# Gate units of the second layer: all 512-column matmuls in a row, then all of 256 columns

## The chip, the cores and the metric

The kernel runs on one core of a Trainium2 chip. The metric is device time in microseconds (us) of one execution. TensorE does matmuls, VectorE (DVE), ScalarE (ACT) and GpSimd (POOL) do elementwise work, and SyncE (SP) issues most DMAs.

## The reference

Two residual layers work on a sequence of 256 positions and 2048 features, with a context of 256 more positions. The first layer mixes with a Fourier transform, the second with windowed attention that also sees the context. Each ends with a gate: the mixed result is multiplied by silu(z), where z is a projection of the layer's normed input, and then projected back.

```python
D_MODEL, SEQ, DEPTH, D_BRANCH = 2048, 256, 2, 4096
def _attention_branch(h, hc, w_in, sink, rows, cols, need_ctx):
    q, k, v, z = jnp.split(h @ w_in, [D_BRANCH, D_BRANCH + kvw, D_BRANCH + 2 * kvw], axis=-1)
    ...
    y = jnp.moveaxis(o, 0, 1).reshape(b, n, D_BRANCH) * jax.nn.silu(z)
...
x = x + gate * (y @ w_out[i])
return _rmsnorm(x, final_g)
```

Here z of the second layer is h (256 x 2048) times the last 4096 columns of w_in.

## The kernel before

All matmuls run in fp32r, a reduced form of fp32. To keep precision, an fp32 operand is split into a high part and a low part (high = cast of the value, low = value minus high), and a product is made from three partial products: high x high, high x low, low x high. The helper `mm3` (lines 78 to 81 of the profile) does this with three matmuls of 512 columns. The helper `half_split`, or `w_cast` and `w_low` apart, split a weight tile of 128 x 1024: ScalarE casts the high part `wh` (L69, in the second layer L1086), VectorE subtracts to get the low part `wl` (L70, L1092).

The second layer is written as a list of units. There are `q` units (queries), `z` units (the gate) and `o` units (the first columns of the output projection). `emit_unit` emits the next unit's matmuls. A gate block `n` (there are 32) makes 128 of the 4096 columns of z for all 256 positions and consists of two `z` units, i = 0 and 1, each over 8 of the 16 tiles of 128 input features. Both units accumulate in one PSUM tile `o[0]` of 128 x 512. The activations `hx1[k]` are 128 x 512: the first 256 columns hold the high part of the 256 positions, the last 256 the low part. So for each k a unit issues two matmuls instead of three. One has wh as its stationary operand and moves all 512 columns (wh x high and wh x low, side by side in PSUM). The other has wl and moves the 256 high columns. `finish_z` later adds the two halves and applies the gate's function.

Matmul by matmul, the unit's loop alternates: k by k first the 512-column one (L1142), then the 256-column one (L1144). Only at the last k of the block is the pair turned, so that the last matmul of the block is the one that covers the whole tile and closes the accumulation.

From the eleventh unit on the order of TensorE, VectorE and ScalarE is written out by hand (`tc.manual_schedule`). A loop runs over 64 attention heads `i`. In it `s_max` (L1182), `s_exp` (L1191), `s_norm` (L1200) and `x_turn` (L1212) are the softmax on VectorE and ScalarE, `s_mm` issues the four score matmuls of the next head (L1173, L1174), `stage_o` the many small matmuls with the values (L1219), and `emit_unit` one or two units per head. `w_cast` and `w_low` prepare weights two to three units ahead. wh and wl share a pool `ws` of six buffers, and three units on, a wh takes the buffer of the wh before. In a group of four gate blocks the fourth block has four transposes (L1015, from `q_turn`) between its two units, in seven of the eight groups; in the other 25 blocks the second unit follows the first without anything between on TensorE. Behind each block stand the four score matmuls.

Behind the loop the remaining output columns are computed. There the order is the scheduler's own, which works with estimated times. `evac` moves a finished PSUM tile out (L1312 to L1314).

Of the kernel before, what the change touches and what calls it, by code (L numbers as in the profile page):

```python
# [16 lines left out]
P = 128  # L17
D = 2048
KT = D // P
DB = 4096  # L20
NB = DB // P
N = 256
# [7 lines left out]
def tile_dit(ctx: ExitStack, tc: tile.TileContext, a: dict, out: bass.AP):  # L30
    nc = tc.nc
    V, S, PE, GP = nc.vector, nc.scalar, nc.tensor, nc.gpsimd
# [8 lines left out]
    def psum():  # L41
        return pp.tile([P, 512], F32, tag="ps", name="ps")
# [35 lines left out]
    def mm3(o, wh, wl, xh, xl, start, stop):  # L78
        PE.matmul(o, wh, xh, start=start, stop=False)  # L79
        PE.matmul(o, wh, xl, start=False, stop=False)  # L80
        return PE.matmul(o, wl, xh, start=False, stop=stop).ins  # L81
# [98 lines left out]
    with tc.tile_pool(name="st", reuse_waits="tile", bufs=1, side="right") as st, ExitStack() as sts:  # L180
# [307 lines left out]
        for i in range(4):  # L488
            for j in range(4):
                k = 4 * i + j  # L490
# [188 lines left out]
    with tc.tile_pool(name="yp", reuse_waits="tile", bufs=32) as ypool:  # L679
# [19 lines left out]
        with tc.tile_pool(name="zp", reuse_waits="tile", bufs=2) as zp:  # L699
# [11 lines left out]
            for kg in range(4):  # L711
# [8 lines left out]
                for j in range(4):  # L720
                    k = kg * 4 + j
                    for b in range(4):
                        wh, wl = w[b // 2]
                        q = slice((b % 2) * 512 + j * P, (b % 2) * 512 + (j + 1) * P)
# [11 lines left out]
            for b in range(NE + 4, NB):  # L736
# [3 lines left out]
                o = psum()  # L740
                for k in range(KT):
                    wh, wl = w[k // 8]
                    q = slice((k % 8) * P, (k % 8 + 1) * P)
# [37 lines left out]
        for i in range(32):  # L781
            sw, kg = i // 16, i % 16
            if kg == 0:
                o = [psum() for _ in range(8)]
# [18 lines left out]
            for j, b in [(j, b) for b in range(8) for j in range(2)] if edge else [(j, b) for j in range(2) for b in range(8)]:  # L803
                q = slice(b * P, (b + 1) * P)
# [21 lines left out]
    o = psum()  # L826
# [12 lines left out]
    o = psum()  # L839
# [17 lines left out]
    for s in range(2):  # L857
        o = psum()[:, 0:N]
# [28 lines left out]
    with tc.tile_pool(name="h1", reuse_waits="tile", bufs=16) as h1p:  # L887
        hx1 = []
        kT = []
        with tc.tile_pool(name="kvp", reuse_waits="tile", bufs=2) as kvp:  # L890
            hc1 = []
            for k in range(KT):
# [3 lines left out]
                for s, h in ((0, hx), (1, hc)):  # L896
                    q = slice(s * N, (s + 1) * N)
# [10 lines left out]
            o = [[psum() for _ in range(2)] for _ in range(4)]  # L908
            for kg in range(8):
                w = [(kv_h, kv_l)] if kg == 0 else ws_split(raw(a["wkv"][kg]))  # L910
                for j in range(2):
                    k = kg * 2 + j
# [3 lines left out]
                    wh, wl = w[j]  # L916
                    for tb in range(4):
                        h = (hx1, hc1)[tb // 2][k]
                        c = (tb % 2) * P
                        for kv in range(2):  # L920
                            q = slice(kv * 512, (kv + 1) * 512)
# [13 lines left out]
            for hp in range(4):  # L935
                o = psum()
# [10 lines left out]
        with tc.tile_pool(name="ye", reuse_waits="tile", bufs=6) as yep, ExitStack() as ats:  # L947
# [23 lines left out]
            def o1_step(k, os_, wh, wl):  # L971
                while len(yh) <= min(k + 2, NB - 1) and (len(yh) < 28 or fin):
                    y_split(len(yh))
                for tb in range(2):
                    mm3(os_[tb], yh[k][:, tb * P : (tb + 1) * P], yh[k][:, N + tb * P : N + (tb + 1) * P], wh, wl, k == 0, k == NB - 1)
# [14 lines left out]
            def finish_q(hk, oq):  # L990
                qr = []
                for tb in range(2):
                    t = act()
                    if hk == 0:
                        roped(t, oq[tb], tb, actp, "act")
                    else:
                        t0 = act()
                        S.copy(t0, oq[tb])
                        roped(t, t0, tb, actp, "act", GP)
                    qr.append(t)  # L1000
                if now[0] < 0:
                    prep_kk(hk)
                    for p2 in range(2):
                        defer.append(lambda p2=p2: q_cast(hk, p2, q_turn(p2, qr)))
                else:
                    posts.append((now[0] + 1, lambda: prep_kk(hk)))
                    for p2 in range(2):
                        turns[now[0] + 2 + p2] = lambda p2=p2: (hk, p2, q_turn(p2, qr))
# [95 lines left out]
            def post(f):  # L1104
                if now[0] < 0:
                    f()
                else:
                    posts.append((now[0] + 1, f))

            def emit_unit():  # L1110
                if pos[0] >= len(ulist):
                    return
                kind, n, i, o = ulist[pos[0]]
                w = ready.pop(pos[0])[:2]
                if pos[0] == 3:
                    kk_hold.append(cast[0])
                pos[0] += 1
                if kind == "o":
                    if n == 0 and i == 0:
                        oA.extend([psum(), psum()])  # L1120
                    for i in range(2):
                        o1_step(n * 2 + i, oA, *(t[:, i * 512 : (i + 1) * 512] for t in w))
                    return
                wh, wl = w
                if kind == "q":
                    if i == 0:
                        o += [psum(), psum()]
                    for j in range(2):
                        k = i * 2 + j
                        q = slice(j * 512, (j + 1) * 512)  # L1130
                        for tb in range(2):
                            mm3(o[tb], hx1[k][:, tb * P : (tb + 1) * P], hx1[k][:, N + tb * P : N + (tb + 1) * P], wh[:, q], wl[:, q], k == 0, k == KT - 1)
                    if i == 7:
                        post(lambda: finish_q(n, o))
                else:
                    if i == 0:
                        o.append(psum())
                    for k in range(i * 8, i * 8 + 8):
                        q = slice((k % 8) * P, (k % 8 + 1) * P)
                        for part in (0, 1) if k < KT - 1 else (1, 0):  # L1140
                            if part == 0:
                                PE.matmul(o[0], wh[:, q], hx1[k], start=k == 0, stop=k == KT - 1)  # L1142
                            else:
                                PE.matmul(o[0][:, 0:N], wl[:, q], hx1[k][:, 0:N], start=False, stop=False)  # L1144
                    if i == 1:
                        post(lambda: finish_z(n, o[0]))

            def finish_z(n, o):
                if n % 4 == 0:
                    szs[n // 4] = at.tile([P, 4, N], F32, tag="th", name="th", bufs=1)  # L1150
                th = szs[n // 4][:, n % 4, :]
                zs = at.tile([P, N], F32, tag="zs", name="zs", bufs=3)
                S.copy(zs, o[:, N : 2 * N])

                def total():
                    V.tensor_tensor(zs, o[:, 0:N], zs, op=ALU.add)
                    S.activation(th, zs, AF.Tanh, scale=0.5)
                    rests.append((now[0] + 1, lambda: V.scalar_tensor_tensor(th, th, 1.0, zs, op0=ALU.add, op1=ALU.mult)))

                second(total)  # L1160
# [69 lines left out]
            for i in range(10):  # L1230
                w_prep(pos[0])
                w_prep(pos[0] + 1)
                emit_unit()
# [12 lines left out]
            with tc.manual_schedule(engines=engines):  # L1246
                for f in defer:
                    f()
                w_cast(pos[0] + 2)
                emit_unit()  # L1250
                w_low(pos[0] + 1)
                s_mm(0)
                w_cast(pos[0] + 2)
                for i in range(64):
# [3 lines left out]
                    if i:  # L1258
                        x_turn(i - 1)
                    emit_unit()  # L1260
                    s_exp(i)
                    run(posts)
# [34 lines left out]
            with tc.tile_pool(name="fin", reuse_waits="tile", bufs=1) as fp:  # L1297
# [40 lines left out]
                o = [[psum() for _ in range(2)] for _ in range(2)]  # L1338
                for kg in range(16):
                    w = ws_split(raw(a["wo1b"][kg]))  # L1340
                    for j in range(2):
                        k = kg * 2 + j
                        wh, wl = w[j]
                        for tb in range(2):
                            for c in range(2):
                                q = slice(c * 512, (c + 1) * 512)
# [4 lines left out]
                o = [psum() for _ in range(2)]  # L1351
# [58 lines left out]
                for j in range(2):  # L1410
                    oh = psum()[:, 0:256]
                    for i, (k, (wh, wl)) in enumerate(held[-4:]):
                        q = slice(j * 256, (j + 1) * 256)
# [106 lines left out]
```

## Time and profile before

| what | value |
|---|---|
| median of 3 runs | 1781.73 us (1780.54 to 1783.49) |
| profiled execution, its own time | 1781.11 us |
| its span, first to last instruction | 1779.3 us |
| TensorE busy | 1757.8 us (99%) |
| VectorE busy | 1375.5 us (77%) |
| ScalarE busy | 880.7 us (49%) |
| granted TensorE clock, mean | 0.998 |
| gate units' first and last matmul | 1154.7 and 1599.6 us |

The span lies inside the profiled execution's time. A busy share is the time in which an engine had an instruction under way. Matmuls overlap: the next one starts before the recorded end of the one before, so the pace of TensorE is read from start to start, not from the durations. PE stands for its matmuls and PEld for its loads of stationary tiles. A row of the timeline has the start, the duration, the engine, the line, the operation, output and inputs by name, the stationary tile's size, the moving columns and a count. In a row of the windows the busy time and count of PE, PEld, DVE, ACT and POOL follow each other. Rows of waits read: engine and line, what it waited for, us in total, times, longest.

### The profile page before, as it was taken

What the parts mean: (1) busy time and instruction counts of PE and PEld (TensorE: products, weight loads), DVE (VectorE), ACT (ScalarE), POOL (GpSimd) and SP (SyncE); (2) the same over time, 40 slices, a digit from 0 to 9 for tenths busy, and PEclk for the clock granted to TensorE, in tenths of its full rate; (3) what the DMA queues carried; (4) which work ended last, traced back from release to release, by engine and by line L of the source; (5) the groups of instructions that cost most, each with busy time, mean ns of one, the idle gap of its engine ahead of it and who ended that gap; (6) DMA issues with size and microseconds to landing.
All of it is one profiled execution on the core that took longest, in us unless ns stands there. A gap on an engine that the chain in (4) does not pass through costs nothing.

```text
span 1779.3 us, 27989 instructions
## 1 busy us (share of the span) xinstructions
PE 1757.8 (99%) x10941; PEld 1480.4 (83%) x10941; DVE 1375.5 (77%) x2314; ACT 880.7 (49%) x1530; POOL 185.3 (10%) x225
## 2 busy tenths in 40 slices
PE   8999999999999999999999999999999999999997
PEld 6669999998888888888888888888888888887886
DVE  5769999978897887687986573788789888977454
ACT  6545444543322233323332443687678777866343
POOL 0001000020000010000000002033213313301010
PEclk9999999999999999999999999999999999999999
DMA  9995655476866676654576333544443444446553
GB/s 388 422 375 171 204 207 200 168 272 225 309 252 247 258 276 257 256 213 166 194 262 229 111 119 115 187 159 142 144 155 143 151 138 162 138 154 249 195 188 120
DMA packets 69028, 370.20 MB, mean 208 GB/s; under 512 B 8736, under 2 KB 10928, under 8 KB 35360
## 3 DMA queue, kind: packets, MB, share of 16 engines
q1 hardware_dynamic: 55344, 328.51, 49.9%
q0 software_dynamic: 9520, 32.96, 5.3%
q10 hardware_dynamic: 4032, 6.95, 1.1%
q8 instruction: 86, 1.41, 0.3%
q14 instruction: 46, 0.38, 0.1%
HBM read 353.16 MB, written 15.21 MB: 207 GB/s over the span
## 4 chain that ended last, share of the span: by engine, by line
PE 97%; DVE 1%; ACT 1%; DMA 1%; issue 0%; SPq 0%; DVEq 0%; ACTq 0%
PE ps L79 26%; PE ps L81 25%; PE ps L80 25%; PE ps L1142 7%; PE ps L1219 4%; PE ps L1144 3%; PE ps L321 2%; PE ps L1173 2%; PE ps L1174 2%; PE ps L1015 0%; DMA xn<-in_x 0%; DMA x1d<-act 0%; PE ps L629 0%; PE ps L600 0%; PE ps L337 0%
## 5 line engine op out<-in xcount | busy, mean ns | idle before, releaser
L69 ACT CAST wh<-raw 128x1024 fp32r<-128x1024 f32 x178 | 187.0, 1054 | 405.3 <-PE ps L80 349.9
L70 DVE TENSOR_TENSOR wl<-raw,wh 128x1024 fp32r<-128x1024 f32 x178 | 219.2, 1232 | 135.2 <-ACT wh L69 134.9
L80 PE MATMUL ps<-hx,wh 128*128 128x512 f32 x700 | 272.3, 389 | 0.0
L79 PE MATMUL ps<-hx,wh 128*128 128x512 f32 x700 | 270.8, 389 | 0.0
L81 PE MATMUL ps<-hx,wl 128*128 128x512 f32 x700 | 270.7, 389 | 0.0
L1092 DVE TENSOR_TENSOR wl<-raw,wh 128x1024 fp32r<-128x1024 f32 x142 | 190.6, 1347 | 56.5 <-ACT wh L1086 55.4
L1086 ACT CAST wh<-raw 128x1024 fp32r<-128x1024 f32 x142 | 148.8, 1049 | 76.0 <-PE ps L80 54.9
L1142 PE MATMUL ps<-h,wh 128*128 128x512 f32 x512 | 184.0, 399 | 0.0
L666 DVE CUSTOM_DVE_ANT_0 raw<-raw,cb 128x1024 f32<-128x1024 f32 x128 | 155.0, 1221 | 34.9 <-DMA raw<-in_adw 34.0
L79 PEld LDWEIGHTS ps<-hx,wh 128*128 128x128 f32 x700 | 131.4, 188 | 27.9 <-ACT hx L406 0.8
L81 PEld LDWEIGHTS ps<-hx,wl 128*128 128x128 f32 x700 | 131.4, 188 | 27.4
L80 PEld LDWEIGHTS ps<-hx,wh 128*128 128x128 f32 x700 | 131.4, 188 | 27.2
L666 DVE CUSTOM_DVE_ANT_0 junk<-raw,cb 128x1024 f32<-128x1024 f32 x96 | 117.2, 1221 | 30.3 <-DMA raw<-in_adw 19.9
L1144 PE MATMUL ps<-h,wl 128*128 128x256 f32 x512 | 138.5, 281 | 0.0
L79 PE MATMUL ps<-wh,h 128*128 128x512 f32 x320 | 124.8, 397 | 1.0 <-ACT h L899 1.0
L80 PE MATMUL ps<-wl,h 128*128 128x512 f32 x320 | 124.6, 389 | 0.0
L81 PE MATMUL ps<-wh,h 128*128 128x512 f32 x320 | 124.4, 390 | 0.0
L1142 PEld LDWEIGHTS ps<-h,wh 128*128 128x128 f32 x512 | 96.2, 188 | 21.3
L1191 ACT ACTIVATE p<-ps,mx 128x512 f32<-128x512 f32 x128 | 86.8, 683 | 53.9 <-DVE mx L1182 53.3
L1144 PEld LDWEIGHTS ps<-h,wl 128*128 128x128 f32 x512 | 96.6, 189 | 2.8
L1182 DVE CUSTOM_DVE_ANT_0 ps<-ps,mask,nsink 128x512 f32<-128x512 f32 x128 | 91.1, 753 | 0.5
L81 PE MATMUL ps<-act,wl 128*128 128x512 f32 x234 | 90.0, 390 | 0.8 <-DVE wl L70 0.8
(367 smaller groups left out, 4007.4 us busy)
## 6 DMA issues: line engine op xcount, KB each, us to landing
raw<-in_adw SPq DMA_DIRECT2D x64, 1024.0 KB, 5.0
raw<-in_wz SPq DMA_DIRECT2D x58, 1024.0 KB, 4.8
raw<-in_awp SPq DMA_DIRECT2D x32, 1024.0 KB, 12.5
raw<-in_wo SPq DMA_DIRECT2D x32, 1024.0 KB, 4.9
raw<-in_wq SPq DMA_DIRECT2D x32, 1024.0 KB, 4.8
raw<-in_wu SPq DMA_DIRECT2D x25, 1016.0 KB, 5.5
raw<-in_wo1b SPq DMA_DIRECT2D x16, 1024.0 KB, 4.8
act<-in_xT POOLq DMA_DIRECT2D x32, 256.0 KB, 5.3
```

The source lines that it names most:

```text
L69: cast[0] = S.copy(h, t[:, i * 1024 : (i + 1) * 1024]).ins
L70: V.tensor_tensor(l, t[:, i * 1024 : (i + 1) * 1024], h.bitcast(F32), op=ALU.subtract)
L79: PE.matmul(o, wh, xh, start=start, stop=False)
L80: PE.matmul(o, wh, xl, start=False, stop=False)
L81: return PE.matmul(o, wl, xh, start=False, stop=stop).ins
L666: V.tensor_tensor_reduce(junk if s == 0 and i < 3 else wf, wf, cb[:, s], 1.0, 0.0, ALU.mult, ALU.add, acc[:, i, kh, fg * 2 + f, s : s + 1])
L1086: cast[0] = S.copy(h, t[:, i * 1024 : (i + 1) * 1024]).ins
L1092: V.tensor_tensor(ready[n][1], ready[n][2], ready[n][0].bitcast(F32), op=ALU.subtract)
L1142: PE.matmul(o[0], wh[:, q], hx1[k], start=k == 0, stop=k == KT - 1)
L1144: PE.matmul(o[0][:, 0:N], wl[:, q], hx1[k][:, 0:N], start=False, stop=False)
L1182: V.tensor_tensor_reduce(so[tb], so[tb], mask[:, tb, :], -0.125, nsink[:, i : i + 1], ALU.add, ALU.min, mx[:, tb : tb + 1])
L1191: S.activation(pt[:, tb, :], so[tb], AF.Exp, bias=mx[:, tb : tb + 1], scale=-1.0, accum_out=sm[:, tb : tb + 1])
```

## The change

In each `z` unit the two kinds of matmul are no longer alternated. The first unit of a block issues its eight 512-column matmuls and then its eight 256-column ones, the second unit the other way round. The matmuls, operands and the PSUM tile are the same, and so are the first and last matmul of a block. With it the line numbers turn: in the changed kernel L1142 is the 256-column matmul and L1144 the 512-column one.

```diff
-                    for k in range(i * 8, i * 8 + 8):
-                        q = slice((k % 8) * P, (k % 8 + 1) * P)
-                        for part in (0, 1) if k < KT - 1 else (1, 0):
-                            if part == 0:
+                    for low in (i, 1 - i):
+                        for k in range(i * 8, i * 8 + 8):
+                            q = slice((k % 8) * P, (k % 8 + 1) * P)
+                            if low:
+                                PE.matmul(o[0][:, 0:N], wl[:, q], hx1[k][:, 0:N], start=False, stop=False)
+                            else:
                                 PE.matmul(o[0], wh[:, q], hx1[k], start=k == 0, stop=k == KT - 1)
-                            else:
-                                PE.matmul(o[0][:, 0:N], wl[:, q], hx1[k][:, 0:N], start=False, stop=False)
```

What stands in a row on TensorE, in the middle of the first plain block, before (h_... are the tiles hx1[k], in the order of k; h_9383 is k = 7, the last of the first unit):

```order
L1142 MATMUL ps<-h_9374,wh 128x512
L1144 MATMUL ps<-h_9374,wl 128x256
L1142 MATMUL ps<-h_9383,wh 128x512
L1144 MATMUL ps<-h_9383,wl 128x256
L1142 MATMUL ps<-h_9392,wh 128x512
L1144 MATMUL ps<-h_9392,wl 128x256
```

And now, on TensorE in the same block, from the first unit's last 512-column matmuls on:

```order
L1144 MATMUL ps<-h_9374,wh 128x512
L1144 MATMUL ps<-h_9383,wh 128x512
L1142 MATMUL ps<-h_9308,wl 128x256
L1142 MATMUL ps<-h_9329,wl 128x256
L1142 MATMUL ps<-h_9338,wl 128x256
L1142 MATMUL ps<-h_9347,wl 128x256
L1142 MATMUL ps<-h_9356,wl 128x256
L1142 MATMUL ps<-h_9365,wl 128x256
L1142 MATMUL ps<-h_9374,wl 128x256
L1142 MATMUL ps<-h_9383,wl 128x256
L1142 MATMUL ps<-h_9392,wl 128x256
L1142 MATMUL ps<-h_9401,wl 128x256
```

The block now reads eight of 512, sixteen of 256 (the last eight are the second unit's), eight of 512.

In a block with transposes between the units, on TensorE before:

```order
L1142 MATMUL ps<-h_9383,wh 128x512
L1144 MATMUL ps<-h_9383,wl 128x256
L1015 MATMUL ps<-ident,act 128x128 x4
L1142 MATMUL ps<-h_9392,wh 128x512
L1144 MATMUL ps<-h_9392,wl 128x256
```

And on TensorE at the same place now:

```order
L1142 MATMUL ps<-h_9374,wl 128x256
L1142 MATMUL ps<-h_9383,wl 128x256
L1015 MATMUL ps<-ident,act 128x128 x4
L1142 MATMUL ps<-h_9392,wl 128x256
L1142 MATMUL ps<-h_9401,wl 128x256
L1142 MATMUL ps<-h_9410,wl 128x256
L1142 MATMUL ps<-h_9419,wl 128x256
L1142 MATMUL ps<-h_9428,wl 128x256
L1142 MATMUL ps<-h_9437,wl 128x256
L1142 MATMUL ps<-h_9446,wl 128x256
L1142 MATMUL ps<-h_9455,wl 128x256
L1144 MATMUL ps<-h_9392,wh 128x512
```

The transposes keep their place between the units; two rows of eight 256-column matmuls now stand around them.

Behind the loop, where the scheduler sets the order, VectorE's order changes at one place, as the first output columns are moved out (numbers of buffers kept, + is the changed kernel):

```order
 L70 TENSOR_TENSOR wl_15907<-raw_15904,wh_15906 128x1024
+L70 TENSOR_TENSOR wl_15911<-raw_15904,wh_15910 128x1024
+L70 TENSOR_TENSOR wl_15941<-raw_15938,wh_15940 128x1024
 L1312 TENSOR_TENSOR act_15856<-ps_14832,gbc_15789 128x512
 L1312 TENSOR_TENSOR act_15861<-ps_14833,gbc_15789 128x512
 L1313 TENSOR_TENSOR act_15791<-act_15791,act_15856 128x512
-L70 TENSOR_TENSOR wl_15911<-raw_15904,wh_15910 128x1024
 L1313 TENSOR_TENSOR act_15799<-act_15799,act_15861 128x512
-L70 TENSOR_TENSOR wl_15941<-raw_15938,wh_15940 128x1024
```

Two weight subtractions now stand ahead of the evacuations. ScalarE's order follows (two casts ahead of L1314), and on TensorE one matmul of the remaining output columns (L79) moves up by six places. GpSimd's and SyncE's orders are the same.

## The prediction

> **What bounds the kernel now.** I read the page first (busy shares, the chain that ended last, the costliest groups), then who waits on TensorE, then the TensorE timeline in the second layer, start by start.
>
> ```profile
> span 1779.3 us, 27989 instructions
> PE 1757.8 (99%) x10941; PEld 1480.4 (83%) x10941; DVE 1375.5 (77%) x2314; ACT 880.7 (49%) x1530; POOL 185.3 (10%) x225
> PE 97%; DVE 1%; ACT 1%; DMA 1%; issue 0%; SPq 0%; DVEq 0%; ACTq 0%
> L1142 PE MATMUL ps<-h,wh 128*128 128x512 f32 x512 | 184.0, 399 | 0.0
> L1144 PE MATMUL ps<-h,wl 128*128 128x256 f32 x512 | 138.5, 281 | 0.0
> ```
>
> TensorE is busy for 99% of the span and the chain that ended last is TensorE for 97%. The two lines of the gate units, 512 matmuls each, have no idle time before them. The waits of TensorE, in full, name neither line:
>
> ```profile
> PE ps L295 <- DMA xn<-in_x: 5.5, 1, 5.5
> PE ps L79 <- ACT dh L260: 2.2, 1, 2.2
> PE ps L79 <- ACT h L899: 1.0, 1, 1.0
> PE ps L81 <- DVE wl L70: 0.8, 1, 0.8
> PE ps L861 <- ACT act L822: 0.4, 1, 0.4
> ```
>
> So the change can act only through the rate at which TensorE itself goes through these 1024 matmuls. "Mean ns of one" (399 and 281) is a latency that overlaps with the next matmul. The rate is the step from one start to the next, and the timeline gives it. Here is a gate block (two units, 32 matmuls) as it is now, from its first pairs to the score matmuls (L1173) behind it:
>
> ```profile
> 1155.09 0.40 PE L1142 MATMUL ps<-h,wh 128*128 128x512 f32 x1
> 1155.32 0.28 PE L1144 MATMUL ps<-h,wl 128*128 128x256 f32 x1
> ...
> 1159.33 0.40 PE L1142 MATMUL ps<-h,wh 128*128 128x512 f32 x1
> ...
> 1161.31 0.39 PE L1142 MATMUL ps<-h,wh 128*128 128x512 f32 x1
> ...
> 1166.95 0.40 PE L1173 MATMUL ps<-kkh,qb 128*128 128x512 f32 x1
> ...
> 1167.87 0.39 PE L1142 MATMUL ps<-h,wh 128*128 128x512 f32 x1
> ```
>
> From 1155.09 to 1159.33 lie twelve pairs: 4.24 / 12 = 0.353 us a pair. The whole block with its four score matmuls repeats after 1167.87 - 1161.31 = 6.56 us. What runs of one width cost is seen near the end of the program, where a row of 512 meets a row of 256 and turns back:
>
> ```profile
> 1756.69 0.39 PE L81 MATMUL ps<-act,ys 128*128 128x512 f32 x1
> ...
> 1758.05 0.39 PE L81 MATMUL ps<-act,ys 128*128 128x512 f32 x1
> 1758.27 0.28 PE L79 MATMUL ps<-wh,ys 128*128 128x256 f32 x1
> ...
> 1759.23 0.28 PE L81 MATMUL ps<-wh,ys 128*128 128x256 f32 x1
> 1759.35 0.63 PE L79 MATMUL ps<-act,ys 128*128 128x512 f32 x2
> 1759.82 0.28 PE L79 MATMUL ps<-wh,ys 128*128 128x256 f32 x1
> ```
>
> Six steps of 512 after 512 take 1758.05 - 1756.69 = 1.36 us, 0.2267 each. Nine of 256 take 1759.35 - 1758.27 = 1.08 us, 0.120 each. The two 512s behind them take 0.47 us, 0.017 more than two at 0.2267. These are the prices I use: a 512 after a 512 is 0.2267, a 256 in a row 0.120, and each turn from 256 to 512 costs 0.017 once. An alternating pair costs 0.353 where one of each from rows of one width costs 0.347: with 0.120 for its 256, the 512 takes 0.233. The loss is at the turns, and the change takes most turns away.
>
> **The change, part by part.** No instruction is added or removed; TensorE's order changes in 64 units.
>
> 1. A plain block (25 of the 32, with nothing between its two units). Now: the period of 6.56 less four score matmuls at 0.2267 (0.907) is 5.653. Changed: eight 512s behind 512s, 8 x 0.2267 = 1.813; then sixteen 256s without a break, since the second unit begins with its 256s: 16 x 0.120 = 1.920; then the turn and eight 512s, 0.017 + 1.813. Sum 5.563. Gain 0.090 a block, 25 x 0.090 = 2.25 us.
>
> 2. A split block (7 of 32), where four transposes (L1015) stand between the two units:
>
> ```profile
> 1174.43 0.39 PE L1142 MATMUL ps<-h,wh 128*128 128x512 f32 x1
> ...
> 1177.24 0.60 PE L1015 MATMUL ps<-ident,act 128*128 128x128 f32 x4
> 1177.59 0.48 PE L1142 MATMUL ps<-h,wh 128*128 128x512 f32 x1
> 1177.91 0.28 PE L1144 MATMUL ps<-h,wl 128*128 128x256 f32 x1
> 1178.03 0.39 PE L1142 MATMUL ps<-h,wh 128*128 128x512 f32 x1
> ...
> 1179.76 0.39 PE L1142 MATMUL ps<-h,wh 128*128 128x512 f32 x1
> ...
> 1180.46 0.39 PE L1173 MATMUL ps<-kkh,qb 128*128 128x512 f32 x1
> ```
>
> Now 1180.46 - 1174.43 = 6.03. The first 512 behind the transposes takes 0.32, 0.09 above its price, and the pairs after it go at (1179.76 - 1178.03) / 5 = 0.346, with no loss. So there is little to win in that half. Changed: 1.813 + 8 x 0.120 + 0.35 for the transposes + a first 256 with the same 0.09 on top (0.21) + 7 x 0.120 + 0.017 + 1.813 = 6.00. Gain 0.03, times 7 is 0.2 us. Whether a 256 pays the same 0.09 the trace doesn't show at this place. From below it pays nothing extra (0.6 us more gain over seven blocks). From above, the 256-column matmul behind a small fp32 row at 32.91 took 0.22, 0.10 extra:
>
> ```profile
> 32.91 0.39 PE L79 MATMUL ps<-dh,xs 128*128 128x256 f32 x1
> 33.13 0.28 PE L80 MATMUL ps<-dl,xs 128*128 128x256 f32 x1
> ```
>
> I take the upper one, since it is the nearer case (a 256 behind fp32 matmuls).
>
> 3. The prepared weights. wh and wl share six buffers, so ScalarE's cast for three units on (L1086) waits for the last 512 of a unit, and VectorE's subtraction (L1092) stands behind casts. The 256s of a second unit now come first, so its wl is wanted 0.24 us earlier against the unit's start, and 0.32 earlier behind the transposes.
>
> ```profile
> 1157.64 1.05 ACT L1086 CAST wh<-raw 128x1024 fp32r<-128x1024 f32 x1 [1.87 <-PE ps L1142]
> 1173.94 2.26 DVE L1092 TENSOR_TENSOR wl<-raw,wh 128x1024 fp32r<-128x1024 f32 x1
> ```
>
> The second row ends at 1176.20 and holds the wl of the split block's second unit, which will be wanted at about 1177.5. That is the tightest place I found, and 1.3 us are left. The other direction helps: the wh of a first unit is read for the last time after 1.8 us of the unit, not 2.8, so the cast of the first row can start about 1 us earlier. A second unit still reads wh last, so that release stays. Nothing comes later. Cost nothing, covered by this 1.3 us; were it gone, TensorE would wait and everything behind it.
>
> 4. The end of the second layer, where VectorE and ScalarE do set the pace for a while:
>
> ```profile
> 1600.00:1605.00 5.00, 5.00 (x24) 4.14 (x23) 5.00 (x12) 4.57 (x9) 0.55 (x1) 1.00 0.54 185
> 1605.00:1622.00 17.00, 16.80 (x79) 12.66 (x85) 16.61 (x33) 14.39 (x33) 3.22 (x6) 1.00 0.69 247
> 1634.00:1770.00 136.00, 134.11 (x603) 111.32 (x602) 73.59 (x79) 54.92 (x66) 11.63 (x7) 1.00 0.47 169
> ```
>
> VectorE (third busy column) fills 5.00 of 5.00 and 16.61 of 17 us there. In the chain of waits this stretch starts at a cast that a matmul released and ends with a matmul:
>
> ```profile
> 1603.45 1.06 ACT wh L1086
> ...
> 1619.34 0.50 PE ps L81
> ```
>
> The release at its head is TensorE's, so the stretch shifts whole and gives nothing back. The steps of TensorE between 1609 and 1620 add up to about 1.0 us above 0.2267 apiece. That is the most that the earlier casts could win (if VectorE enters the stretch ahead), and the last four blocks' gain, 4 x 0.090 = 0.4 us, is the most that a full VectorE could take back. I take 0 and keep -0.4 and +1.0 for the range.
>
> 5. In the last stage two subtractions (L70) now stand ahead of the evacuation of the first output columns (L1312), and ScalarE's order follows. The third window above shows VectorE busy for 73.59 of 136 us, and no wait of TensorE there but the 0.8 on L70. Nothing on TensorE waits for these evacuations until the end, so 0.
>
> Sum: 2.25 + 0.2 = 2.5 us. The profiled execution took 1781.11 us around its span of 1779.3 (1.8 us lie outside, and stay), so it would take 1778.6. The median shown is 1781.73, 0.6 above; from it, **1779.2 us**. That is 0.14% less, inside the 0.2% which is about what a measurement of this kernel can tell from no change.
>
> **The rivals.**
>
> *More than that.* Half of a 512's 0.2267 is 0.1133. If the 256s in rows of sixteen went at that, and VectorE entered the last stretch ahead, the gain would be 2.5 + 512 x 0.0067 + 1.0 = 6.9 us at most; with half of these additions it is 4.7, which gives 1777.0. Against it: the nine 256s quoted sit at 0.120, and the stretch begins with a release by TensorE.
>
> *Order is no matter.* If a step depended on its own columns alone, the 0.353 would be what a 512 and a 256 cost anywhere, and the time would stay at 1781.7. Against it: the same 512 columns take 0.2267 in a row and 0.233 behind a 256. For it: the 0.346 pairs behind the transposes show that alternation need not lose, so part of the loss may be a matter of phase. The Trainium skill, "TensorE: Matmul & The Clock Gate", section "Back-to-back issue gap", gives a gap that depends on the columns alone (N / 2.4 + 2.5 ns, which by that page would be 216 and 109 ns); by it no order gains anything. The trace disagrees with 0.233 against 0.2267 for equal widths.
>
> *Slower: weight loads no longer hidden.* Each matmul has a stationary tile of its own, and its load starts with the matmul before it:
>
> ```profile
> 1158.86 0.19 PEld L1142 LDWEIGHTS ps<-h,wh 128*128 128x128 f32 x1
> 1158.98 0.19 PEld L1144 LDWEIGHTS ps<-h,wl 128*128 128x128 f32 x1
> ```
>
> A load is recorded with 0.19 us, longer than a 256 step. In pairs every second matmul is a long one that could take up a late load; in a row of sixteen none is. If the row fell to a load per 0.19, 512 x 0.07 = 36 us would be lost: 1815. It decides from the point where 2.5 us are eaten: 2.5 / 512 = 0.005, a step of 0.125. Against it: 0.120 over nine in a row, with loads of the same 128 x 128 form.
>
> *Slower: wl late.* If VectorE were more than 1.3 us later than in the trace at a second unit, each microsecond of it would be paid up to 32 times. Nothing in the change makes it later.
>
> **How the numbers follow.** Forecast 0.64, more than that 0.14, no matter 0.14, load-bound rows 0.05, wl late 0.03. Faster by over 0.2% means below 1778.2: all of "more", and the part of the forecast in which the ends of points 2 and 4 or the scatter of a median (runs from 1780.5 to 1783.5) add 1.0 us, 0.08: together 0.22. Slower by over 0.2%: the last two, less the part that only eats the gain, 0.06. The rest, 0.72, is the same. The range takes the nearer half of "more" and all of "no matter": 1777.0 to 1781.7.
>
> **What would show it.** Timeline of a plain block: eight 512 starts 0.227 apart, sixteen 256 starts 0.120 apart, the two 512s behind them 0.017 above their price, and a block period of 6.47 instead of 6.56. "Mean ns of one" of the 512 line falls from 399 to about 390, while the 256 line stays near 282. No new row in TensorE's waits. The gain up to 1600 us is 2.5 us, and what lies behind it shifts whole. Wrong if the 256 rows step at 0.125 or more, if the 512s keep 0.233, or if a wait on L1092 appears before a second unit.

## The result, and the profile after

The changed kernel takes 1774.88 us, the median of 6 runs (1774.12 to 1776.34), against 1781.71 (1780.54 to 1783.85, 6 runs) before. The ratio is 0.9965, 95% interval 0.9956 to 0.9975. So it is faster by 0.35%, and outside the predicted range. The profiled spans differ by 6.4 us. The page after, its TensorE totals, its chain and the two groups of the gate units:

```profile
span 1772.9 us, 27988 instructions
PE 1751.8 (99%) x10941; PEld 1477.6 (83%) x10941; DVE 1376.2 (78%) x2314; ACT 880.9 (50%) x1530; POOL 187.2 (11%) x225
PE 97%; DVE 1%; ACT 1%; DMA 0%; issue 0%; SPq 0%; DVEq 0%
L1144 PE MATMUL ps<-h,wh 128*128 128x512 f32 x512 | 127.3, 391 | 0.0
L1142 PE MATMUL ps<-h,wl 128*128 128x256 f32 x512 | 68.1, 284 | 0.0
```

Nothing in these lines tells where 6.4 us went: the chain is TensorE's for 97% as before, and the mean latencies, 391 and 284 ns, are within 2 of the forecast (390 and 282). Nor do the waits of TensorE; no row on L1092 came, and L899 fell from 1.0 to 0.2:

```profile
PE ps L295 <- DMA xn<-in_x: 6.0, 2, 5.8
PE ps L79 <- ACT dh L260: 2.2, 1, 2.2
PE ps L81 <- DVE wl L70: 0.8, 1, 0.8
PE ps L861 <- ACT act L822: 0.4, 1, 0.4
PE ps L79 <- ACT h L899: 0.2, 1, 0.2
```

So I read the second layer's timeline start by start again, this time all of it. In each group of eight heads TensorE does the matmuls with the values (`stage_o`, L1219) in two bursts of 128 small matmuls, with one query unit between them. They are in plain fp32, as the transposes are, and not in fp32r as the opening has it for all matmuls. In the changed kernel, a plain gate block with the first matmuls of the next one, and then a first burst with what follows it on TensorE:

```profile
1161.05 1.98 PE L1144 MATMUL ps<-h,wh 128*128 128x512 f32 x8
1162.86 2.08 PE L1142 MATMUL ps<-h,wl 128*128 128x256 f32 x16
1164.77 2.00 PE L1144 MATMUL ps<-h,wh 128*128 128x512 f32 x8
1166.61 0.39 PE L1173 MATMUL ps<-kkh,qb 128*128 128x512 f32 x1
1167.52 0.62 PE L1144 MATMUL ps<-h,wh 128*128 128x512 f32 x2
...
1254.34 3.73 PE L1219 MATMUL ps<-pall,vr 32*64 32x256 f32 x128
1258.00 0.50 PE L79 MATMUL ps<-wh,h 128*128 128x512 f32 x1
```

And the same burst before the change, with the second burst of the pair behind it:

```profile
1255.58 4.28 PE L1219 MATMUL ps<-pall,vr 32*64 32x256 f32 x128
1259.78 0.50 PE L79 MATMUL ps<-wh,h 128*128 128x512 f32 x1
...
1262.73 3.71 PE L1219 MATMUL ps<-pall,vr 32*64 32x256 f32 x128
1266.37 0.50 PE L79 MATMUL ps<-wh,h 128*128 128x512 f32 x1
```

The block's period is 1167.52 - 1161.05 = 6.47 us, as forecast. The burst, which the change doesn't touch, took 1259.78 - 1255.58 = 4.20 us before and takes 1258.00 - 1254.34 = 3.66 now. The second one took 1266.37 - 1262.73 = 3.64 even before. From starts to starts, over the whole layer:

| stretch of TensorE | before | after | difference, us |
|---|---|---|---|
| start of the first gate block | 1154.75 | 1154.57 | 0.18 |
| 25 plain blocks with their score matmuls, each | 6.560 | 6.473 | 2.17 |
| 7 split blocks with theirs, each | 6.940 | 6.900 | 0.28 |
| first burst of a pair, seven | 4.20 to 4.32 | 3.66 to 3.84 | 3.8 |
| second burst of a pair, seven | 3.64 | 3.64 | 0 |
| behind the last gate block, to the end | 179.49 | 179.48 | 0.0 |

The sum, 6.4 us, is the difference of the spans. The gate blocks give the forecast 2.45 us. More than half comes from the seven first bursts. One trace of it is in the waits of the weight loads (PEld), which I had not read. Before:

```profile
PEld ps L1219 <- issue: 4.9, 14, 0.4
PEld ps L1219 <- ACT p L1191: 0.9, 4, 0.2
PEld ps L1219 <- PE ps L80: 0.4, 1, 0.4
```

After:

```profile
PEld ps L1219 <- issue: 4.9, 14, 0.4
PEld ps L1219 <- PE ps L80: 0.4, 1, 0.4
```

The row that is gone names ScalarE's exponentials (L1191), whose reading of the scores frees the PSUM tiles that the burst writes. It shows 0.9 of the 3.8 us; the rest are slow steps, each too short to be listed as a wait. The second exponential of the head at that burst, before and then after:

```profile
1255.06 0.68 ACT L1191 ACTIVATE p<-ps,mx 128x512 f32<-128x512 f32 x1
```

```profile
1253.28 0.68 ACT L1191 ACTIVATE p<-ps,mx 128x512 f32<-128x512 f32 x1
```

It ended 1255.74 - 1255.58 = 0.16 us behind the burst's start, and now ends 0.38 us ahead of it. So ScalarE's chain gained more than TensorE did, and the question for the experiments was where.

### The profile page after: what moved, and what is told of

The parts are those of the page before. It is cut to its first block, busy times and chain, and to the rows that moved or that the text cites. A ratio compares the mean times of both kernels' runs of the same rounds, so it can differ in the third digit from the quotient of the medians.

```text
span 1772.9 us, 27988 instructions
## 1 busy us (share of the span) xinstructions
PE 1751.8 (99%) x10941; PEld 1477.6 (83%) x10941; DVE 1376.2 (78%) x2314; ACT 880.9 (50%) x1530; POOL 187.2 (11%) x225
## 3 DMA queue, kind: packets, MB, share of 16 engines
q8 instruction: 86, 1.41, 0.3%
## 4 chain that ended last, share of the span: by engine, by line
PE 97%; DVE 1%; ACT 1%; DMA 0%; issue 0%; SPq 0%; DVEq 0%
PE ps L79 26%; PE ps L81 26%; PE ps L80 26%; PE ps L1144 7%; PE ps L1142 3%; PE ps L1219 3%; PE ps L321 2%; PE ps L1173 2%; PE ps L1174 2%; DMA xn<-in_x 0%; PE ps L1015 0%; PE ps L629 0%; PE ps L600 0%; PE ps L337 0%; DVE wl L1092 0%
## 5 line engine op out<-in xcount | busy, mean ns | idle before, releaser
L79 PE MATMUL ps<-hx,wh 128*128 128x512 f32 x700 | 270.8, 389 | 0.0
L1092 DVE TENSOR_TENSOR wl<-raw,wh 128x1024 fp32r<-128x1024 f32 x142 | 191.2, 1352 | 56.3 <-ACT wh L1086 55.5
L79 PEld LDWEIGHTS ps<-hx,wh 128*128 128x128 f32 x700 | 131.4, 188 | 28.0 <-ACT hx L406 0.8
L1144 PE MATMUL ps<-h,wh 128*128 128x512 f32 x512 | 127.3, 391 | 0.0
L79 PE MATMUL ps<-wh,h 128*128 128x512 f32 x320 | 124.7, 396 | 0.2 <-ACT h L899 0.2
L1191 ACT ACTIVATE p<-ps,mx 128x512 f32<-128x512 f32 x128 | 86.8, 683 | 52.9 <-DVE mx L1182 52.8
L1144 PEld LDWEIGHTS ps<-h,wh 128*128 128x128 f32 x512 | 94.1, 188 | 18.2
L80 PE MATMUL ps<-act,wh 128*128 128x512 f32 x234 | 90.7, 389 | 0.0
L79 PE MATMUL ps<-act,wh 128*128 128x512 f32 x234 | 89.6, 389 | 0.0
```

The costliest lines, as they stand in the source:

```text
L1092: V.tensor_tensor(ready[n][1], ready[n][2], ready[n][0].bitcast(F32), op=ALU.subtract)
L1191: S.activation(pt[:, tb, :], so[tb], AF.Exp, bias=mx[:, tb : tb + 1], scale=-1.0, accum_out=sm[:, tb : tb + 1])
```

## The experiments

All were timed against the kernel before, five rounds each; its median in the four sets of runs was 1781.20, 1781.03, 1781.05 and 1781.83 us. "Group" is the time from the first gate block of a group of four to that of the next: 60.80 to 60.94 us before, 59.95 to 60.18 after. "Burst" is the length of the first bursts. Each edit is one line about the order of a unit's matmuls, written as a list; `rows` is the changed order and `alt` the order before:

```diff
+rows = [(k, low) for low in (i, 1 - i) for k in range(i * 8, i * 8 + 8)]
+alt = [(k, low) for k in range(i * 8, i * 8 + 8) for low in ((0, 1) if k < KT - 1 else (1, 0))]
+for k, low in ...:   # which of the two, below
```

**One half of the change.** The first units alone, and the second units alone.

```diff
+for k, low in rows if i == 0 else alt:    # first_only
+for k, low in rows if i == 1 else alt:    # second_only
```

> Only the first unit of each gate block is put in rows (eight 512s, then eight 256s); the second alternates as before. Theory A (the first unit's wh is read for the last time 1 us earlier, ScalarE's next cast and then its exps run ahead, and the seven first bursts of value matmuls no longer wait): bursts of 3.65 to 3.85 us instead of 4.2 to 4.3 (3.8 us in all), plus 32 x 0.05 = 1.6 us of turns: 5.4 us faster than before, 1776.3. Theory B (the lead comes from the second unit's wl, whose last read is 1.8 us earlier): the turns alone, 1.6 us, 1780.1, bursts at 4.2 to 4.3.

> Only the second unit of each gate block is put in rows (eight 256s, then eight 512s); the first alternates as before. Theory A: bursts stay at 4.2 to 4.3 us; 25 x 0.034 us of turns, 0.8 us faster at most, 1780.9. Theory B: bursts fall to 3.7, 4.6 us faster, 1777.1.

Both win on the gate blocks: periods of 6.52 and 6.51 instead of 6.56. first_only took 1778.40 us, ratio 0.9982 (0.9973 to 0.9991), burst 4.05, group 60.50. second_only took 1781.09 us, 0.9999 (0.9990 to 1.0008), burst 4.33 to 4.46, group 60.8 to 60.9. The second one is the telling miss: its three plain blocks are 0.05 us shorter each in a group, its bursts 0.13 longer, and the group is as long as before. A shorter TensorE stretch gains nothing there; something else sets the group's length. The first units move it, by 0.3 to 0.4 us a group.

**Which buffer comes free.** The first unit gives wh back late, as before the change, but wl early; the second unit as in the change.

```diff
+for k, low in rows if i == 1 else [(0, 0)] + [(k, 1) for k in range(8)] + [(k, 0) for k in range(1, 8)]:    # late_wh
```

> The second unit as in the change; the first unit issues one 512, eight 256s, then seven 512s, so that wh is read until the unit's end, with one more turn a block. Theory A: bursts stay at 4.2 to 4.3 us or wait longer, the blocks gain 0.067 us each (period 6.49), 1.8 us faster, 1779.9. Theory B: bursts at 3.7, 5.6 us faster, 1776.1.

It took 1775.49 us, 0.9965 (0.9952 to 0.9977): all of the gain, with bursts of 3.64 and groups of 60.05 but for the first, 3.74 and 60.14. The theory that the gain hangs on wh's early release fell. The cast in the same group shows why (L1141 is the 256-column matmul in this kernel's numbering):

```profile
1215.86 1.05 ACT L1086 CAST wh<-raw 128x1024 fp32r<-128x1024 f32 x1 [0.28 <-PE ps L1141]
```

The cast waits for a wl's last read. wh and wl share the pool, and the cast takes the buffer that is given back first, whichever it was.

**One block of the four.** The change in the fourth block only, in the second only, and in all but the second.

```diff
+for k, low in rows if n % 4 == 3 else alt:    # fourth_only
+for k, low in rows if n % 4 == 1 else alt:    # second_block
+for k, low in alt if n % 4 == 1 else rows:    # not_second
```

> The change in every fourth gate block alone (8 of 32, the last of each group, the seven with transposes among them); the others alternate. Theory A, in the form that ScalarE runs on its own from the last cast that a gate block releases: nearly all of the burst gain, 3.7 us, and 0.4 us of turns, 4.1 us faster, 1777.6. A rival in which the lead adds up over the four blocks of a group: about a quarter of 3.8, so 1.3 us faster in all, 1780.4.

> The change in the second gate block of each group of four alone (8 of 32 blocks). Theory C (VectorE runs without a pause from that block to the first burst of value matmuls; its start is set by the cast that waits for the first of the two weight buffers to come free in that block's first unit): the cast goes from 9.45 to 8.5 us behind the group's start, the seven first bursts from 4.2 to 4.3 us down to 3.65 to 3.85, a group from 60.9 to 60.2 to 60.3: 4.5 us faster than before, 1776.7. Rival D (the lead has to be gathered in every block): no more than a quarter of the changed kernel's gain, 1.7 us, 1779.5.

> The change in all gate blocks but the second of each group (24 of 32). Theory C: the cast in the second block stays at 9.35 to 9.45 us behind the group's start, bursts stay at 4.3 to 4.5, a group at 60.8: 0.9 us faster than before at most, 1780.3. Rival D: three quarters of the changed kernel's gain, 5 us, 1776.2.

fourth_only took 1781.78 us, 1.0001 (0.9992 to 1.0010), burst 4.25 to 4.38. second_block took 1780.64 us, 0.9997 (0.9988 to 1.0006), burst 4.29 to 4.44. not_second took 1776.26 us, 0.9971 (0.9960 to 0.9983), burst 3.85, group 60.2. So neither the fourth nor the second block alone moves the group. second_block did bring VectorE some 0.4 us ahead, but lost it a few us on, in a subtraction that took 1.93 us in the kernel before and takes 1.2 elsewhere:

```profile
1350.85 2.33 DVE L1092 TENSOR_TENSOR wl<-raw,wh 128x1024 fp32r<-128x1024 f32 x1 [0.27 <-ACT wh L1086]
```

GpSimd was at work then, on the rotation of the queries. Its work begins behind a chain that starts in the first block, which led to the next runs.

**The first block.** The change in the first block only, and in all but the first.

```diff
+for k, low in rows if n % 4 == 0 else alt:    # first_block
+for k, low in alt if n % 4 == 0 else rows:    # not_first
```

> The change in the first gate block of each group of four alone (8 of 32 blocks). Theory E (the weight buffer that the first block's first unit frees early lets ScalarE cast earlier and then copy the queries earlier; GpSimd starts their rotation earlier and is done earlier, and VectorE's subtractions, which take 1.6 to 2.3 us instead of 1.2 while GpSimd works, are over earlier): GpSimd starts 5.2 us behind the group's start instead of 6.1, bursts of 3.85 to 4.05 us instead of 4.2 to 4.3, a group of 60.3 to 60.6 instead of 60.9, 2 to 4 us faster than before, 1777.2 to 1779.2. If only a lead gathered over all blocks counts: under 1 us, 1780.5.

> The change in all gate blocks but the first of each group (24 of 32). Theory E: GpSimd starts at 6.1 as before, bursts stay at 4.3 to 4.5, groups at 60.8 to 60.9, at most 0.6 us faster than before, 1780.6. If the lead is gathered by the number of blocks: 4.5 us faster, 1776.7.

first_block took 1778.36 us, 0.9988 (0.9979 to 0.9997), with bursts of 4.04 and groups of 60.55 to 60.59. not_first has three of the four blocks changed and took 1780.29 us, 0.9995 (0.9986 to 1.0004), with bursts of 4.39 to 4.53 and groups as before. The chain is seen in the timelines of ScalarE, GpSimd and VectorE. Before, in the group that starts at 1215.69:

```profile
1218.58 1.05 ACT L1086 CAST wh<-raw 128x1024 fp32r<-128x1024 f32 x1 [1.79 <-PE ps L1142]
1221.05 1.07 ACT L998 COPY act<-ps 128x512 f32<-128x512 f32 x2
1221.78 2.04 POOL L879 TENSOR_TENSOR act<-act,rope 128x512 f32<-128x512 f32 x1 [13.71 <-ACT act L998]
1233.29 2.66 POOL L987 TENSOR_TENSOR kkl<-act,kkh 64x512 fp32r<-64x512 f32 x2
1234.89 2.15 DVE L1092 TENSOR_TENSOR wl<-raw,wh 128x1024 fp32r<-128x1024 f32 x1
1237.63 1.21 DVE L1092 TENSOR_TENSOR wl<-raw,wh 128x1024 fp32r<-128x1024 f32 x1
```

After, in the same group, which starts at 1214.75:

```profile
1216.77 1.05 ACT L1086 CAST wh<-raw 128x1024 fp32r<-128x1024 f32 x1 [0.91 <-PE ps L1144]
1219.24 1.07 ACT L998 COPY act<-ps 128x512 f32<-128x512 f32 x2
1219.97 2.05 POOL L879 TENSOR_TENSOR act<-act,rope 128x512 f32<-128x512 f32 x1 [12.82 <-ACT act L998]
1231.50 2.66 POOL L987 TENSOR_TENSOR kkl<-act,kkh 64x512 fp32r<-64x512 f32 x2
1233.09 2.16 DVE L1092 TENSOR_TENSOR wl<-raw,wh 128x1024 fp32r<-128x1024 f32 x1
1235.84 1.21 DVE L1092 TENSOR_TENSOR wl<-raw,wh 128x1024 fp32r<-128x1024 f32 x1
```

Behind the group's start the cast begins at 2.89 us before and 2.02 after, since ScalarE waits for the first unit to free a buffer. The copy of the queries (L998) follows at 5.36 and 4.49, GpSimd's 14 us of work at 6.09 and 5.22, and the last subtraction of the rows at 21.94 and 21.09. That subtraction is the first full-speed one behind GpSimd. Each is 0.85 to 0.87 us earlier, and the exponential at the burst, 39.37 and 38.53 us behind the start, by 0.84.

**GpSimd made lighter.** In these two GpSimd leaves out the sine part of the queries' rotation, so that part of the result is missing. One has the order before, one the changed order.

```diff
     def roped(dst, src, tb, pool, tag="rt", eng=V):
         ...
+        if eng is GP: return    # behind the cosine part
```

> The gate units alternate as before; GpSimd leaves out the sine part of the queries' rotation (four of six operations a group), so that it works 5 us a group instead of 14. Theory E: VectorE's subtractions in the gate blocks fall from 1.6 to 2.3 us to 1.2, VectorE is ahead at the bursts, these fall to 3.65 to 3.85 us, 4 to 4.4 us faster than before, 1777. If the casts' release alone sets VectorE's pace: no change, 1781.2.

> The changed kernel with the same part left out on GpSimd. Theory E: its bursts wait for almost nothing any more, so only 0 to 1 us faster than the changed kernel, 1774 to 1775; the two gains are the same gain. If they were separate: 1770.5.

light_gp took 1779.51 us, 0.9989 (0.9980 to 0.9998), with bursts of 4.04 and groups of 60.65; less than a release of VectorE by itself should give. Three of its rows:

```profile
1348.33 1.20 DVE L1092 TENSOR_TENSOR wl<-raw,wh 128x1024 fp32r<-128x1024 f32 x1
1354.89 1.21 DVE L1092 TENSOR_TENSOR wl<-raw,wh 128x1024 fp32r<-128x1024 f32 x1
1358.56 1.05 ACT L1086 CAST wh<-raw 128x1024 fp32r<-128x1024 f32 x1 [1.23 <-PE ps L1142]
```

The subtractions are at 1.2 us again, and VectorE is ahead. Then a cast waits 1.23 us for a matmul of the fourth block's first unit, 1358.56 - 1335.99 = 22.57 us behind the group's start. That is a second release, behind which the first one's gain can't pass. In first_block, where the fourth block is as before, the same cast begins 22.49 us behind the start and the burst has the same 4.04. In the changed kernel it comes at 21.52.

rows_light_gp took 1774.24 us, 0.9964 (0.9951 to 0.9976), with all bursts at 3.64 and all groups at 59.95. The exponentials end 0.55 us ahead of the burst. After the change, then, a lighter chain wins 0.6 us of median at most: TensorE's own 59.95 us is the floor, and the changed kernel's groups are within 0.23 of it.

**The two blocks together.** If the first and the fourth block hold the releases, these two alone must give nearly all that the bursts gained.

```diff
+for k, low in rows if n % 4 in (0, 3) else alt:               # first_fourth
+for k, low in rows if n % 4 in (0, 3) and i == 0 else alt:    # first_fourth_u0
```

> The change in the first and the fourth gate block of each group (16 of 32 blocks). Theory F (three releases in a row hold VectorE and ScalarE back: G1, the first block's first unit, 2.9 us behind the group's start, which sets when GpSimd starts; G2, the fourth block's first unit, 22.6 us; G3, the fourth block's second unit, 25.5 us; the later one counts): both blocks together give what neither gives alone, bursts of 3.85 to 3.95 us, a group of 60.3 to 60.4 instead of 60.9, 4 us faster than before, 1777. If each block's part adds up on its own: the first block's 2.7 us and the fourth's 0, so 1778.4.

> The same in the first units of these blocks alone; second units alternate. Theory F: G1 and G2 move, G3 stays at 25.5 us, so VectorE loses 0.3 us there, bursts of 4.05, a group of 60.55, 2.7 us faster than before, 1778.3. If G1 and G2 were all: as with whole blocks, 1777.

first_fourth took 1776.35 us, 0.9970 (0.9959 to 0.9981), with groups of 60.22 to 60.31 and this burst, 1381.09 - 1377.34 = 3.75:

```profile
1377.34 3.82 PE L1219 MATMUL ps<-pall,vr 32*64 32x256 f32 x128
1381.09 0.50 PE L79 MATMUL ps<-wh,h 128*128 128x512 f32 x1
```

first_block gained 0.3 us a group and fourth_only nothing; together they give 0.62, of which only 0.13 is the shorter gate blocks. That is what two releases in series do. first_fourth_u0, with the first units alone, took 1778.71 us, 0.9985 (0.9976 to 0.9994), burst 4.05, group 60.57. So the second units of the two blocks carry 0.33 us a group as well. VectorE's timeline shows where most of it is lost. In first_fourth, in the group that starts at 1337.57, and then in first_fourth_u0, in the same group, which starts at 1335.97:

```profile
1342.47 1.21 DVE L1092 TENSOR_TENSOR wl<-raw,wh 128x1024 fp32r<-128x1024 f32 x1
```

```profile
1341.53 3.72 DVE L1092 TENSOR_TENSOR wl<-raw,wh 128x1024 fp32r<-128x1024 f32 x2 [0.57 <-PE ps L1142]
```

The subtraction starts 4.90 us behind the group's start where the second unit is changed too. With the first units alone it starts at 5.56, behind a wait for a 256-column matmul (L1142) of the first block's second unit, and runs into GpSimd's work. From 12 us behind the start on, GpSimd and VectorE are both about 0.26 us later. The other 0.08 is added at a subtraction 25.6 us behind the start, where the expectation had put all of the loss; no wait is listed there. In first_only the first of these waits is the same 0.57 us, and at the second place a wait is listed, 1360.81 - 1335.30 = 25.51 us behind the group's start:

```profile
1360.81 1.23 DVE L1092 TENSOR_TENSOR wl<-raw,wh 128x1024 fp32r<-128x1024 f32 x1 [0.18 <-PE ps L1141]
```

Against the changed kernel, VectorE loses 0.24 us at the first place and 0.30 at the second, which is what this group is longer by (60.50 against 59.95). So the second units hold two releases of their own, which count once the first units' have moved.

**The burst moved away from the exponentials.** The unit that stands between the two bursts goes ahead of both, in the order before and in the changed one.

```diff
-                        stage_o(oo, 0)
                         emit_unit()
+                        stage_o(oo, 0)
                         stage_o(oo, 1)
```

> The kernel before, its gate units alternating, with the query unit that stood between the two halves of the value matmuls now ahead of both: TensorE has 2.7 us of other work while the exps end. Theory C: TensorE no longer waits at the first burst, 7 x 0.63 = 4.4 us faster than before, 1776.8, though no gate unit is touched. If the slow bursts were the bursts' own pace: no change, 1781.2.

> The changed kernel with the query unit ahead of both halves of the value matmuls. Theory C: of TensorE's waits only 0.1 us a group is left to take, so 0.7 us faster than the changed kernel, 1774.2, and no sum of the two gains (the change's 6.4 and the move's 4.4 would give 1770.5 if they were separate).

o_later took 1781.65 us, 1.0001 (0.9992 to 1.0009), and rows_o_later 1776.83 us, 0.9971 (0.9959 to 0.9982): no gain from it in either. Yet the exponentials now end about 2.5 and 3.0 us ahead of the burst, and undisturbed groups take 59.83 and 59.53 us. With the wait gone, the change is worth the difference of 0.30 us a group, which is what its four gate blocks give (3 x 0.087 + 0.04). What ate it is another stall. The two bursts are one of 256 matmuls now, 7.09 us where undisturbed, but up to 10.35 in o_later and 9.28 in rows_o_later. TensorE's waits in the two kernels name it only as issue:

```profile
PE ps L1219 <- issue: 2.9, 3, 2.0
```

```profile
PE ps L1219 <- issue: 3.3, 4, 1.6
```

The stops of 0.5 to 2.35 us lie at the 195th to 250th matmul of a burst. In the two groups where both kernels have one, it is at the same matmul, the 250th and the 236th, so they hang on the place in the program. The profile shows no semaphore for them. It does show a DMA queue of the kind "instruction" (q8), which moves blocks of 16 KB. Here is the longest stop in o_later, by the weight loads (PEld), and what that queue began to move between 1384.10 and 1385.20:

```profile
1382.95 1.24 PEld L1219 LDWEIGHTS ps<-pall,vr 32*64 32x64 f32 x45
1386.63 0.90 PEld L1219 LDWEIGHTS ps<-pall,vr 32*64 32x64 f32 x19 [2.43 <-issue]
```

```profile
q8 instruction: 1, 0.02, 5.0%
```

That block landed at 1385.05, and the next matmul started 1.57 us later. There are ten stops of 0.46 us or more: four in each of these two kernels, and one each in late_wh and fourth_only, in the burst of 256 that every kernel has behind the loop. Each ended 1.25 to 1.62 us behind the landing of such a block. In the kernel before, the queue moves 86 blocks for 21882 matmuls and weight loads, about 64 bytes for each (1.41 MB). So it fits that TensorE waits for its own instructions. As no run changes how they are loaded, this is argued and not shown. The burst behind the loop takes 7.5 to 7.8 us instead of 7.09 in five kernels (first_fourth_u0, light_gp, not_first, late_wh, fourth_only), so 0.4 to 0.7 us of their profiled spans comes from there and not from the gate units.

**All runs side by side.** The burst's length against the end of the last exponential ahead of it, counted from the burst's start, for eight of the kernels:

| kernel | exponential's end, us | burst, us |
|---|---|---|
| not_first | +0.35 to +0.48 | 4.39 to 4.53 |
| before | +0.16 to +0.28 | 4.20 to 4.32 |
| first_block, light_gp | -0.01 to +0.01 | 4.04 to 4.05 |
| not_second | -0.11 to -0.21 | 3.84 to 3.93 |
| first_fourth | -0.22 to -0.30 | 3.74 to 3.83 |
| after | -0.20 to -0.39 | 3.66 to 3.84 |
| rows_light_gp | -0.56 | 3.64 |

The burst ends 4.04 us behind the exponential, or takes its own 3.64, whichever is later. In the kernel before, this made the group's period a loop: the group's first unit frees a buffer, ScalarE, GpSimd and VectorE work through their 37 us (the exponential ends 40.05 us behind the group's start, the first cast starts at 2.89), the exponentials free the burst's PSUM, and TensorE ends the burst and goes on to the next group. Ahead of the burst, TensorE's share of that loop is only the time to the release.

## Why the prediction was wrong

- **The opening premise failed.** "So the change can act only through the rate at which TensorE itself goes through these 1024 matmuls" was drawn from the waits of PE alone. The 3.8 us lay in slow steps inside seven bursts, of which only the 0.9 in the waits of PEld is listed. They came from ScalarE's exponentials, which freed the burst's PSUM too late. The kernel before showed them otherwise too: of two bursts of 128 equal matmuls, the first took 4.2 to 4.3 us and the second 3.64.
- **Point 3 failed, the term that was mis-sized.** It said that a first unit's cast can start about 1 us earlier, and the cast did, by 0.87 us. It priced this at "Cost nothing" and saw no gain, as nothing seemed to wait for it. It was worth 3.8 us. A detail was wrong as well: a cast does not need the buffer of an earlier wh, it takes the first one given back (late_wh). And "A second unit still reads wh last, so that release stays" missed that the second unit's wl comes free earlier, which is worth 0.33 us a group (first_fourth against first_fourth_u0).
- **Points 1 and 2 held.** 2.25 and 0.2 us were forecast, 2.17 and 0.28 came. In the timeline of the gate block above the steps are 1.81 / 8 = 0.226 and 1.91 / 16 = 0.119. The turn from 256 to 512 costs 0.027 us, not 0.017 (1166.61 - 1164.77 = 1.84 for eight), since it is spread over five steps and the prediction's place had two. The 0.233 for a pair's 512 was a remainder, with 0.120 taken for its 256. By the starts in the kernel before, a pair's 512 takes 0.2365 us on average and its 256 0.117. Their sum is 0.353 all the same, so the gain stands. The first 256 behind the transposes takes 0.204, where 0.21 was taken.
- **Points 4 and 5 held.** What lies behind the last gate block shifted whole, 179.49 to 179.48 us. "The gain up to 1600 us is 2.5 us" failed with point 3: it is 6.4.
- **The rivals.** "More than that" gave 6.9 us at most and so comes near the number, by a mechanism that did not happen: only the first 256 of a row takes 0.113, the others 0.119 to 0.120, and the last stretch gave nothing. "Order is no matter" fell with the blocks' 0.087. The Trainium skill, "TensorE: Matmul & The Clock Gate", section "Back-to-back issue gap", gives the gap by columns alone for a matmul by itself, and says that in a stream loads and matmuls set the spacing together. By columns alone, no block could have become shorter. "Slower: weight loads no longer hidden" did not happen at its price: no step in the rows of sixteen 256s is above 0.120, where a load per step would have made it 0.19. Whether the 0.0067 us by which 0.120 exceeds the row's first step is the loads', no run here separates. No wl was late.

## What to carry to other kernels

An engine that is busy 99% and hardly listed as waiting can still be paced by others, as TensorE was here, through steps that are each too short to be listed. Compare stretches of equal work on it (here the first and the second burst of 128), and read the waits of its weight loads too. Where an order of matmuls is changed, ask which buffers it gives back earlier, and follow that release to the end of the loop. A gain behind one release shows only when the next one in series moves with it.

## What the runs showed of the hardware

A VectorE subtraction of 128 x 1024 (L1092) takes 1.20 us alone and 1.6 to 2.4 while GpSimd works; with GpSimd's sine part left out, the subtractions at that place went back to 1.2. It goes the other way too. In light_gp a pair of GpSimd's L987 took 4.07 us beside subtractions of 1.2, against 2.66 in the kernel before:

```profile
1348.88 4.07 POOL L987 TENSOR_TENSOR kkl<-act,kkh 64x512 fp32r<-64x512 f32 x2 [2.51 <-ACT kkh L985]
```

The Trainium skill, "SBUF — State Buffer", section "Who interferes with whom", says that a VectorE instruction with two inputs in SBUF contends with a GpSimd instruction that reads SBUF, and that the order of issue decides which of the two is held up. The rows agree. For VectorE's two-port modes that page of the Trainium skill says that the later one is blocked for the whole of the other instruction. The runs show the same for this subtraction. In the rows of the kernel before above, GpSimd's pair ends at 1235.95, and the subtraction that starts at 1234.89, 1.06 us ahead of that, takes 2.15 us, 0.95 more than alone. In the gate stretches of all 16 kernels 406 subtractions began while a GpSimd instruction was under way, and each took 1.21 us and what was left of that instruction, less 0.12 to 0.14. The 120 that began ahead of the GpSimd instruction took 1.20 to 1.23. Then GpSimd pays, as at the start of the rotation in the same group:

```profile
1221.47 1.21 DVE L1092 TENSOR_TENSOR wl<-raw,wh 128x1024 fp32r<-128x1024 f32 x1
```

GpSimd's L879 starts at 1221.78, 0.90 us ahead of the end of this row, and takes 2.04 us, where the same operation takes 1.29 with no subtraction beside it.

The step of a matmul depends on the one before it. A 512 takes 0.2267 us behind another 512. A 512 and a 256 together take 0.353 us in pairs, and 0.2267 + 0.120 = 0.347 in rows; behind the transposes pairs took 0.346 too. The loss was 0.087 us a plain block.
